# All attention values in one Strassen stage, through DRAM, in a hybrid decoder layer

## The chip, the cores and the metric

The kernel runs on one core of one Trainium2 chip. The metric is the time of one execution on the device in microseconds (us), lower is better. Beside plain timed runs there is one execution recorded by the hardware profiler, from which all rows below come. Its engines are PE (TensorE; PEld is its weight load), DVE (VectorE), ACT (ScalarE), POOL (GpSimd) and SP (SyncE, which issues most DMAs).

## The reference

One decoder layer on 1024 tokens of 1024 channels, float32. The part that matters here is the combined projection and the two attentions that read it:

```python
h = rms_norm(x, pre_mix_g[l])
proj = h @ w_in[l]
qa, ka, va, qb, kb, vb, gates = jnp.split(proj, split_at, axis=-1)
...
oa = diff_attention(qa, ka, va, lam)             # A: 4 heads, values 4 x 128 columns
oa = rms_norm(oa, diff_head_g[l]) * (1.0 - lam_init)
...
for g, (window, dil) in enumerate(B_PAIRS):      # B: 3 groups of 4 heads, values 3 x 512 columns
    o_g, lse_g = dilated_group(qb[:, :, g], kb[:, :, g], vb[:, :, g], window, dil)
...
mix = (g_a * ya + g_b * yb) @ w_mix_out[l]
x = x + rms_norm(mix, post_mix_g[l])
h = rms_norm(x, pre_ffn_g[l])                    # then a conv-gated MLP and a last residual
```

The values `va` and `vb` are 512 + 1536 = 2048 columns of `h @ w_in`: a product of 1024 x 1024 by 1024 x 2048.

## The kernel before, in words

Every float32 operand of a product is split into two fp32r parts, high and low: `split` writes the high part with a copy on ACT (whi, xh, t2h and so on) and the low part, source minus high, on DVE (wlo, xl, t2l). A product is then three matmuls, high by high, low by high and high by low (`mm3`), summed in PSUM. `xh` and `xl` hold the normalized input, transposed, as 8 blocks of 128 channels by 1024 tokens.

The stages, in order of time: three gate columns while x arrives (the "first" gates); the norm's factors `rstd`, their row form `rstd_row`, and the rotation tables; two more gate columns; the values of attention A's first head pair (`proj_v`, 65 to 87 us); query and key of head 0 (`proj_a`); attention A head by head (about 118 to 450 us); attention B in 12 steps of one (head pair, group, head) each (450 to 930); the output products; the mix; the MLP's up products, most by Strassen's scheme with seven products in place of eight; and the down products, likewise.

In the attentions a head is cut in blocks of 128 queries. A block makes scores (PE into PSUM `s`), takes the maximum with a mask (DVE), the exponential (ACT), combines (DVE), is transposed (PE into `pt`), split again (ACT, DVE) and multiplied with the values `vh`, `vl` (PE into `o`). Jobs that are due a block or two later are put off by `later`. Between these jobs, `interleave` spreads "fills", PE work that waits for nothing of the attention: the projections of the next head (`p`, in B `proj_b`), gate columns (`g`), and pieces of the value products (`v`, `w`, `V`, and in B the two halves of `values_of`). The strings in `A_FILLS` say which fills each of A's four heads gets. A head half of A closes with `head_norm`: PE sums squares into `o`, DVE computes a root and writes `spread`, PE transposes `spread` into `pt`, and DVE multiplies `osb` by that.

`proj_v` makes 256 columns at a time, token block by token block: 8 blocks of 8 x 3 matmuls of 256 columns. For A, and for B's group 0, the result goes straight from PSUM into `vh` and `vl`. For groups 1 and 2, whose keys are read with a stride, it goes through DRAM (`v_d`) and comes back permuted (`vperm`).

What sets the order: the code is written in the order of the stages, and a scheduler with a timeline of its own puts the instructions into each engine's queue, by priority and by when it takes operands to be there. Each engine then runs its queue strictly in order. PSUM has eight banks: `acc` has 3, `s` and `pt` 2 each, `o` 1. A gate column (`gate`, `put_gate`) is two half products of 24 matmuls into `acc`; DVE empties each with a multiply by `rstd_row`, and the result is stored to DRAM.

Of the kernel before, what the change touches and what calls it, by code (L numbers as in the profile page):

```python
# [24 lines left out]
P = 128  # L25
S = 1024
# [23 lines left out]
START_GATES, A_FILLS, B_GATES = 2, ("pggg", "pvgg", "wpgg", "PVg"), 3  # L50
# [8 lines left out]
def plan():  # L59

    order = [("t", GT + i * P) for i in FIRST_GATES]
    for pair in range(2):
        for h in (2 * pair, 2 * pair + 1):
            order += [("t", QA + h * P), ("t", KA + h * P)]
            if h % 2 == 0:
                order += [("v", VA + pair * 256, i) for i in range(2)]
    for pair in range(2):
        for g in range(BG):
            order += [("v", VB + g * 512 + pair * 256, i) for i in range(2)]
            for h in (2 * pair, 2 * pair + 1):  # L70
                order += [("t", QB + g * 512 + h * P), ("t", KB + g * 512 + h * P)]
    order += [("t", GT + i * P) for i in range(2 * KC) if i not in FIRST_GATES]
    return order
# [15 lines left out]
def trunk(ctx: ExitStack, tc: tile.TileContext, a, out):  # L89
# [28 lines left out]
    def load_raw(src):  # L118
        raw = raws_in[-1].tile([P, 512], F32, tag="raw", name="raw")
        dma(raw, src)  # L120
        return raw
# [71 lines left out]
    v_d = dram.tile([4, S, 256], F32, name="v_d")  # L193
# [15 lines left out]
    def proj_t(col, evacuate):  # L209

        wh, wl = load_unit(w_in[where[("t", col)]])
        for half, sl in enumerate(halves()):
            ps = psum()
            for k in range(KC):
                w = slice(k * P, (k + 1) * P)
                mm3(ps, wh[:, w], wl[:, w], xh[:, k, sl], xl[:, k, sl], k == 0, k == KC - 1)
                if k == KC - 1:
                    evacuate(half, sl, ps)
                if k % 2:
                    yield 0.5  # L220

    def put_gate(i, sl, ps):
        t = rt.tile([P, 512], F32, tag="t2", name="gate")
        nc.vector.tensor_tensor(t, ps, rstd_row[:, sl], op=ALU.mult)
        nc.scalar.dma_start(gt_d[i][:, sl], t)

# [46 lines left out]
    rt = open_pool(attn, "rt", side="right", bufs=2)  # L273
    raws_in.append(rt)
    ps_s = open_pool(attn, "ps_s", bufs=2, space=PSUM)
    ps_o = open_pool(attn, "ps_o", space=PSUM)
    tabs = open_pool(attn, "tabs", side="right")
    rstd_row = tabs.tile([P, S], F32, name="rstd_row")
    slots = open_pool(attn, "slots", side="right")
# [38 lines left out]
    with ExitStack() as st0:  # L318
# [6 lines left out]
        def load_first(c0, c1):  # L325
            for n, i in enumerate(FIRST_GATES):
                dma(raws[n][:, c0:c1], w_in[where[("t", GT + i * P)]][:, c0:c1])
# [73 lines left out]
        cos_a, sin_a = load_tabs(64, 32)  # L401
# [24 lines left out]
    def v_tiles(i):  # L426
        return [slot(t, (P, 4, 256)) for t in ("vh", "vl")]

    def proj_v(col, res, wk=None, via=None, dil=1, ms=range(8)):

        us = [load_unit(w_in[where[("v", col, i)]]) for i in range(2)]
        for m in ms:
            ps = psum()[:, :256]
            tk = slice(m * P, (m + 1) * P)
            for k in range(KC):
                wh, wl = us[k // 4]
                w = slice((k % 4) * 256, (k % 4 + 1) * 256)
                nc.tensor.matmul(ps, xh[:, k, tk], wh[:, w], start=k == 0, stop=False)  # L438
                nc.tensor.matmul(ps, xl[:, k, tk], wh[:, w], start=False, stop=False)  # L439
                nc.tensor.matmul(ps, xh[:, k, tk], wl[:, w], start=False, stop=k == KC - 1)  # L440
                if k == KC // 2 - 1:
                    yield 0.5
            r = rstd[:, m : m + 1]
            if via is None:
                if m % 4 == 0:
                    res.append(v_tiles(m // 4))
                h, l = (t[:, m % 4] for t in res[-1])
                nc.scalar.activation(h, ps, AF.Copy, scale=r)
                nc.vector.scalar_tensor_tensor(l, ps, r, h.bitcast(F32), op0=ALU.mult, op1=ALU.subtract)
            else:  # L450
                if m % 2 == 0:
                    vr = wk.tile([P, 2, 256], F32, tag="vraw", name="vraw", bufs=2)
                nc.scalar.activation(vr[:, m % 2], ps, AF.Copy, scale=r)
                if m % 2:
                    nc.scalar.dma_start(via.rearrange("(m p) c -> p m c", p=P)[:, m - 1 : m + 1], vr)
            yield 0.5
        if via is not None:
            n = S // dil // P
            src = via.rearrange("(ih p r) c -> p r ih c", r=dil, ih=n)
            for i in range(2):  # L460
                v = slot("vperm", (P, 4 // n, n, 256), F32)
                for ih in range(n):
                    dma(v[:, :, ih], src[:, i * 4 // n : (i + 1) * 4 // n, ih])
                h, l = v_tiles(i)
                split(h, l, v.rearrange("p r ih c -> p (r ih) c"))
                res.append((h, l))
# [160 lines left out]
    free_gates = [i for i in range(2 * KC) if i not in FIRST_GATES]  # L627

# [32 lines left out]
    def values_of(pair, g):  # L661
        col = VB + g * 512 + pair * 256
        if g == 0:
            return proj_v(col, vs_b[pair, g])
        return proj_v(col, vs_b[pair, g], wk_b[0], v_d[pair * 2 + g - 1], DIL[g])
# [5 lines left out]
    with st_a:  # L671
        ops = [[] for _ in range(AH)]
        vs = [[] for _ in range(AH // 2)]
        run(gates(START_GATES)[0])
        run(proj_v(VA, vs[0]))
        run(proj_a(0, ops[0]))
        for h in range(AH):
# [4 lines left out]
                "v": lambda: (proj_v(VA + 256, vs[1], ms=range(4)), 4),  # L682
                "w": lambda: (proj_v(VA + 256, vs[1], ms=range(4, 8)), 4),
                "g": lambda: gates(1),
                "P": lambda: (proj_b(0, 0, ops_b[steps[0]]), 8),
                "V": lambda: (values_of(0, 0), 8),
# [177 lines left out]
    for n, (pair, g, h) in enumerate(steps[:-1]):  # L864
# [3 lines left out]
        if h % 2 == 0 and n + 2 < len(steps):  # L868
            ahead = values_of(*steps[n + 2][:2])
            fills.append((itertools.islice(ahead, 8), 4))  # L870
        elif h % 2:
            fills.append((ahead, 4))
# [219 lines left out]
    tt = {}  # L1092

    def new_sum(name, x, ys, eng=None):

        t = tt[name] = sums.tile([P, 4, 512], F32, tag=name, name=name)
        f = lambda v: v.bitcast(F32)
# [9 lines left out]
    def split_sum(name, to=None):  # L1107

        to = to or [xw.tile([P, 4, 512], F32R, tag=name + p, name=name + p) for p in "hl"]
        pieces.extend(functools.partial(split, *(t[:, k] for t in to), tt[name][:, k]) for k in range(4))  # L1110
# [3 lines left out]
    with ExitStack() as st_s:  # L1114
# [5 lines left out]
        new_sum("t2", b22, tt["t1"])  # L1120
        new_sum("t4", b21, tt["t2"])
# [122 lines left out]

    def tt(o, x, y, op=ALU.subtract):
        nc.vector.tensor_tensor(o, x, y, op=op)
# [175 lines left out]
def layout(inp):  # L1422
# [10 lines left out]
    for u in plan():  # L1433
        if u[0] == "t":
            us.append(units(w[:, u[1] : u[1] + P], KC, P))
        else:
            us.append(units(w[u[2] * 512 : (u[2] + 1) * 512, u[1] : u[1] + 256], 4, 256))
    arr["w_in"] = np.stack(us)
    for n in ("w_a_out", "w_b_out"):
        arr[n] = np.stack([units(f[n][0][:, i * 256 : (i + 1) * 256], 4, 256) for i in range(4)])  # L1440
# [28 lines left out]
```

## Time and profile before

| | us |
|---|---|
| runs, median of 3 (lowest to highest) | 1772.2 (1769.66 to 1774.67) |
| profiled execution, its own time | 1767.12 |
| its span, first to last instruction | 1765.3 |
| PE busy in the span | 1721.8 |
| DVE busy | 1329.9 |
| ACT busy | 865.3 |

Busy time is the time in which at least one of the engine's instructions was running. A row of the timeline has the start of an instruction, how long it ran, engine, line, operation, and output and inputs by the program's names; a bracket at its end tells how long the engine stood before it and what released it. A row of groups has the count, the busy time, the mean of one in ns, and the idle time ahead of the group. Rows of stages have the busy time of each engine with its number of instructions, then the clock that PE was granted (1.00 is full), then DMA's share and GB/s.

### The profile page before, as it was taken

The page shows a single profiled execution, that of the slowest core. Times are in us where ns is not written, and L with a number is a line of the kernel's source. Part 1 is how long each engine was busy: PE and PEld are TensorE (multiplying, and loading weights), DVE is VectorE, ACT ScalarE, POOL GpSimd, SP SyncE. Part 2 cuts the span into 40 slices and gives each one's busy share as a digit, 9 for nine tenths or more (in the row PEclk, how much of TensorE's full clock was granted, in tenths as well). Part 3 has the DMA queues.
Part 4 walks back from the last instruction along what each step waited for, and adds up shares of the span by engine and source line. Part 5 has one row for each costly group of instructions (what it writes and reads, how often), then busy time and mean ns, then how long its engine had stood idle before and what let it go on. Part 6 is the DMA issues. An engine that isn't in the chain of part 4 may idle for free.

```text
span 1765.3 us, 24106 instructions
## 1 busy us (share of the span) xinstructions
PE 1721.8 (98%) x8754; PEld 1459.4 (83%) x8754; DVE 1329.9 (75%) x2612; ACT 865.3 (49%) x1585; POOL 51.6 (3%) x78
## 2 busy tenths in 40 slices
PE   9999999999999999999999999999999999999997
PEld 7987788789888888888877878878888888888886
DVE  4667786776556667565665867799999999789978
ACT  6375464644455645465652533364444444355452
POOL 0000000000000000000000410300000000000000
PEclk9999999999999999999999999999999999999999
DMA  8411112211121335221376533023222222196624
GB/s 271 162 60 42 54 55 72 78 55 59 56 86 60 102 97 156 75 88 55 126 254 222 166 131 108 37 72 107 90 78 95 78 78 96 60 342 216 206 77 155
DMA packets 100407, 197.61 MB, mean 112 GB/s; under 512 B 16368, under 2 KB 23216, under 8 KB 100288
## 3 DMA queue, kind: packets, MB, share of 16 engines
q1 hardware_dynamic: 92192, 185.06, 31.4%
q10 hardware_dynamic: 8096, 11.01, 1.7%
q8 instruction: 68, 1.11, 0.3%
q14 instruction: 51, 0.42, 0.1%
HBM read 152.37 MB, written 43.66 MB: 111 GB/s over the span
## 4 chain that ended last, share of the span: by engine, by line
PE 78%; DVE 9%; DMA 7%; issue 3%; ACT 3%; SPq 1%; POOL 0%; DVEq 0%; ACTq 0%
PE acc L148 15%; PE acc L147 15%; PE acc L149 15%; PE acc L438 3%; PE acc L440 3%; PE acc L439 3%; PE acc L1301 3%; PE acc L1300 3%; PE acc L1302 3%; PE acc L990 2%; PE acc L991 2%; PE acc L989 2%; PE o L484 2%; PE pt L472 1%; DMA og<-og_d 1%
## 5 line engine op out<-in xcount | busy, mean ns | idle before, releaser
L147 PE MATMUL acc<-xh,whi 128*128 128x512 f32 x744 | 296.3, 399 | 4.7 <-DVE t L421 2.6
L148 PE MATMUL acc<-xh,wlo 128*128 128x512 f32 x744 | 296.9, 399 | 1.4 <-DVE wlo L140 1.4
L149 PE MATMUL acc<-xl,whi 128*128 128x512 f32 x744 | 294.6, 398 | 0.0
L143 ACT ACTIVATE whi<-raw 128x512 fp32r<-128x512 f32 (+1 forms) x258 | 158.8, 624 | 208.5 <-PE acc L149 125.2
L140 DVE TENSOR_TENSOR wlo<-raw,whi 128x512 fp32r<-128x512 f32 (+1 forms) x255 | 185.0, 732 | 47.3 <-ACT whi L143 45.8
L147 PEld LDWEIGHTS acc<-xh,whi 128*128 128x128 f32 x744 | 140.6, 189 | 33.6 <-ACT xh L342 3.2
L148 PEld LDWEIGHTS acc<-xh,wlo 128*128 128x128 f32 x744 | 140.8, 189 | 29.2 <-DVE wlo L140 1.6
L149 PEld LDWEIGHTS acc<-xl,whi 128*128 128x128 f32 x744 | 141.2, 190 | 28.7
L147 PE MATMUL acc<-mh,whi 128*128 128x512 f32 x400 | 156.5, 391 | 1.9 <-ACT whi L143 1.7
L148 PE MATMUL acc<-mh,wlo 128*128 128x512 f32 x400 | 156.3, 391 | 0.2 <-DVE wlo L140 0.2
L149 PE MATMUL acc<-ml,whi 128*128 128x512 f32 x400 | 156.1, 391 | 0.0
L438 PE MATMUL acc<-whi,xh 128*128 128x256 f32 x512 | 147.4, 288 | 0.0
L440 PE MATMUL acc<-wlo,xh 128*128 128x256 f32 x512 | 146.8, 287 | 0.0
L439 PE MATMUL acc<-whi,xl 128*128 128x256 f32 x512 | 146.7, 287 | 0.0
L420 ACT ACTIVATE t<-acc 64x512 f32<-64x512 f32 (+1 forms) x160 | 94.6, 591 | 44.8 <-PE acc L149 42.4
L1175 DVE TENSOR_TENSOR u<-acc,u 128x512 f32<-128x512 f32 x133 | 90.6, 685 | 25.7 <-PE acc L149 25.6
L143 ACT ACTIVATE whi<-s 128x512 fp32r<-128x512 f32 x76 | 47.2, 628 | 105.2 <-PE acc L149 96.0
L439 PEld LDWEIGHTS acc<-whi,xl 128*128 128x128 f32 x512 | 97.7, 191 | 0.7
L438 PEld LDWEIGHTS acc<-whi,xh 128*128 128x128 f32 x512 | 97.8, 191 | 0.6
L440 PEld LDWEIGHTS acc<-wlo,xh 128*128 128x128 f32 x512 | 97.7, 191 | 0.5
L147 PEld LDWEIGHTS acc<-mh,whi 128*128 128x128 f32 x400 | 75.5, 189 | 18.2 <-ACT whi L143 2.1
L148 PEld LDWEIGHTS acc<-mh,wlo 128*128 128x128 f32 x400 | 75.5, 189 | 16.2 <-DVE wlo L140 0.5
(313 smaller groups left out, 3867.4 us busy)
## 6 DMA issues: line engine op xcount, KB each, us to landing
raw<-in_w_in SPq DMA_DIRECT2D x126, 256.0 KB, 2.7
raw<-in_w_up SPq DMA_DIRECT2D x88, 256.0 KB, 2.6
raw<-c_d SPq DMA_DIRECT2D x48, 256.0 KB, 3.5
c_d<-c SPq DMA_DIRECT2D x22, 512.0 KB, 2.7
raw<-in_w_down SPq DMA_DIRECT2D x37, 256.0 KB, 3.6
gl<-gt_d SPq DMA_DIRECT2D x16, 512.0 KB, 5.8
gt_d<-gate ACTq DMA_DIRECT2D x26, 256.0 KB, 2.0
og_d<-osb SPq DMA_DIRECT2D x12, 512.0 KB, 4.4
```

The lines of the kernel that those rows point to most:

```text
L140: eng.tensor_tensor(lo, src, hi.bitcast(F32), op=ALU.subtract)
L143: nc.scalar.activation(hi, src, AF.Copy)
L147: nc.tensor.matmul(o, sh, mh, start=first, stop=False)
L148: nc.tensor.matmul(o, sl, mh, start=False, stop=False)
L149: nc.tensor.matmul(o, sh, ml, start=False, stop=last)
L420: nc.scalar.activation(t1[dst], ps[src], AF.Copy)
L438: nc.tensor.matmul(ps, xh[:, k, tk], wh[:, w], start=k == 0, stop=False)
L439: nc.tensor.matmul(ps, xl[:, k, tk], wh[:, w], start=False, stop=False)
L440: nc.tensor.matmul(ps, xh[:, k, tk], wl[:, w], start=False, stop=k == KC - 1)
L1175: nc.vector.tensor_tensor(to, made(p), x, op=ALU.add)
L1300: nc.tensor.matmul(banks[m], gh[:, tk], wh, start=f == 0, stop=False)
L1301: nc.tensor.matmul(banks[m], gl[:, tk], wh, start=False, stop=False)
```

## The change

All 2048 value columns are made in one stage, after the first gates and four more gate columns (two before) and ahead of attention A. The stage is the product of 1024 tokens by 1024 channels by 1024 columns, twice (`cp` 0 and 1), each by Strassen's scheme: seven products of 512 x 512 x 512 in place of eight. Each is 4 x 4 x 3 matmuls of 512 columns, into four banks at once.

The x side of the seven products needs four combinations of x's quarters. `less` and `less_sum` compute T1 to T4 on DVE ahead of the four gates; T2 to T4 get places of their own, T1 is put into the quarter `b12` of `xh`, `xl` once the gates have read it, and that quarter is loaded again late in the stage. The weight side is combined on DVE as it arrives (`ready_v`) from a second layout of the weights, `w_v`. `take_v` adds the products up in SBUF (`yv`), `stored` scales by `rstd` and stores to `v_d`. Before each use, `values` loads four pieces of 128 x 2 x 256 from `v_d` and splits them. So a fill `v`, `w` or `V` now holds no PE work, and its weight is 0. The fills of A become pgg, pvg, wpg, PVgg in place of pggg, pvgg, wpgg, PVg. The load of A's rotation tables moves behind the stage, and `rt`, the pool of raw weights and rotation temporaries (2 buffers of each), is opened behind it.

```diff
-START_GATES, A_FILLS, B_GATES = 2, ("pggg", "pvgg", "wpgg", "PVg"), 3
+START_GATES, A_FILLS, B_GATES = 4, ("pgg", "pvg", "wpg", "PVgg"), 3
...
-    v_d = dram.tile([4, S, 256], F32, name="v_d")
+    v_d = dram.tile([S, 2048], F32, name="v_d")
...
-    def proj_v(col, res, wk=None, via=None, dil=1, ms=range(8)):
-
-        us = [load_unit(w_in[where[("v", col, i)]]) for i in range(2)]
-        for m in ms:
-            ps = psum()[:, :256]
...
+    def less(o, x, y, d):
+
+        tt(o, f32(x[0]), f32(y[0]))
+        tt(d, f32(x[1]), f32(y[1]))
+        tt(o, o, d, ALU.add)
+
+    def less_sum(o, x, y):
+
+        tt(o, f32(x[0]), y)
+        tt(o, o, f32(x[1]), ALU.add)
+
+    temps = open_pool(st_r, "temps", side="right")
+    t1_raw = [temps.tile([P, 512], F32, tag=f"t1{k}", name="t1") for k in range(4)]
+    for k in range(4):
+        x11, x12, x21, x22 = ([t[:, k] for t in b] for b in (b11, b12, b21, b22))
+        d, e, o = (temps.tile([P, 512], F32, tag=n, name=n) for n in "deo")
+        less(t1_raw[k], x12, x11, d)
+        less_sum(e, x22, t1_raw[k])
+        split(t2[0][:, k], t2[1][:, k], e)
+        less(o, x22, x12, d)
+        split(t3[0][:, k], t3[1][:, k], o)
+        less_sum(e, x21, e)
+        split(t4[0][:, k], t4[1][:, k], e)
+    todo = [free_gates.pop(0) for _ in range(START_GATES)]
+    for i in todo:
+        for _ in gate(i):
+            pass
+
+    for k in range(4):
+        split(*(t[:, k] for t in b12), t1_raw[k])
+    t1 = b12
...
+        order_v = (("p1", b11), ("p5", t1), ("p6", t2), ("p7", t3), ("p3", b22), ("p2", b21), ("p4", t4))
+        todo = [(cp, p, x, k) for cp in range(2) for p, x in order_v for k in range(4)]
...
+        def stored(y, cp, i, j, m):
+
+            tb = j * 4 + m
+            nc.scalar.activation(y, y, AF.Copy, scale=rstd[:, tb : tb + 1])
+            nc.scalar.dma_start(v_d[tb * P : (tb + 1) * P, cp * 1024 + i * 512 : cp * 1024 + (i + 1) * 512], y)
...
+        for n, (cp, p, x, k) in enumerate(todo):
+            while fetched < min(n + 8, len(todo)):
+                fetch_v(fetched)
+                fetched += 1
+            while made < min(n + 5, len(todo)):
+                ready_v(made)
+                made += 1
...
+            for m in range(4):
+                tk = slice(m * P, (m + 1) * P)
+                mm3(banks[m], x[0][:, k, tk], x[1][:, k, tk], wh, wl, k == 0, k == 3)
+            if k == 3:
+                for m in range(4):
+                    take_v(cp, p, m, banks[m])
...
+    def values(col, dil, res, pieces=range(4)):
+
+        n = S // dil // P
+        src = v_d[:, col : col + 256].rearrange("(ih p r) c -> p r ih c", r=dil, ih=n)
+        for i in pieces:
+            if i % 2 == 0:
+                res.append([slot(t, (P, 4, 256)) for t in ("vh", "vl")])
+            raw = load_raw(src[:, i * 2 // n : (i + 1) * 2 // n, 0] if n == 1 else src[:, i * 2 // n, 2 * i % n : 2 * i % n + 2])
+            split(*(t.rearrange("p b c -> p (b c)")[:, i % 2 * 512 : (i % 2 + 1) * 512] for t in res[-1]), raw)
+            yield 0
...
-        run(gates(START_GATES)[0])
-        run(proj_v(VA, vs[0]))
+        run(values(0, 1, vs[0]))
         run(proj_a(0, ops[0]))
...
-            fills.append((itertools.islice(ahead, 8), 4))
+            fills.insert(0, (itertools.islice(ahead, 2), 0))
```

What this does to the queues is seen at three places.

DVE near the start, up to the first multiply that frees a bank of the free gates. L385 and L387 (L384 and L386 after) write `rstd` and `rstd_row`, the other rows of L29x and L30x are the rotation tables. Before:

```order
L385 COPY edge<-rxy 128x8
L296 TENSOR_SCALAR ang<-ang,edge 128x1024
L387 COPY rstd_row<-edge 128x1024
L298 TENSOR_SCALAR kk<-ang 128x1024
L299 TENSOR_SCALAR kk<-kk 128x1024
L300 SCALAR_TENSOR_TENSOR sin<-kk,ang 128x1024
L140 TENSOR_TENSOR wlo<-raw,whi 128x512
L301 SCALAR_TENSOR_TENSOR sin<-kk,sin 128x1024
L302 SCALAR_TENSOR_TENSOR sin<-kk,sin 128x1024
L140 TENSOR_TENSOR wlo<-raw,whi 128x512
L224 TENSOR_TENSOR gate<-acc,rstd_row 128x512
```

After; L432 is `tt`, `e` and `t_484` are T sums, L136 splits them:

```order
L432 TENSOR_TENSOR e<-xh,t_484 128x512
L299 SCALAR_TENSOR_TENSOR cos<-kk,ang 128x1024
L384 COPY edge<-rxy 128x8
L432 TENSOR_TENSOR e<-e,xl 128x512
L300 SCALAR_TENSOR_TENSOR cos<-kk,cos 128x1024
L386 COPY rstd_row<-edge 128x1024
L136 TENSOR_TENSOR t2l<-e,t2h 128x512
L301 SCALAR_TENSOR_TENSOR cos<-kk,cos 128x1024
L432 TENSOR_TENSOR e<-xh,e 128x512
L303 TENSOR_SCALAR cos<-cos 128x1024
L395 SCALAR_TENSOR_TENSOR neg<-sin,pt 128x512
L220 TENSOR_TENSOR gate<-acc,rstd_row 128x512
```

`rstd_row` and the first multiply now come behind nearly all the T sums and behind the table of the cosine, which stood after the multiply.

DVE where the values end and the first query projection begins. L421 (L419) is the first operation on the finished query product; `wlo` ahead of it are that product's weights. Before:

```order
L449 SCALAR_TENSOR_TENSOR vl<-acc,edge,vh 128x256 x6
L140 TENSOR_TENSOR wlo<-raw,whi 128x512 x2
L449 SCALAR_TENSOR_TENSOR vl<-acc,edge,vh 128x256
L140 TENSOR_TENSOR wlo<-raw,whi 128x512 x2
L421 TENSOR_TENSOR t_914<-acc,cos 128x512
```

After; the `yv` rows are the additions of the stage's last two products:

```order
L432 TENSOR_TENSOR yv<-acc,yv 128x512 x3
L432 TENSOR_TENSOR yv<-o,yv 128x512
L432 TENSOR_TENSOR yv<-s,yv 128x512 x2
L432 TENSOR_TENSOR yv<-pt,yv 128x512 x2
L136 TENSOR_TENSOR vl<-raw,vh 128x512 x4
L136 TENSOR_TENSOR wlo<-raw,whi 128x512 x6
L419 TENSOR_TENSOR t_2227<-acc,cos 128x512
```

Two splits of the query's weights stood ahead of the last value evacuation; now all of them stand behind the last product's additions and behind four splits of values.

PE at the end of a head of A (head 1), up to the transposes of `spread` that close its first head half. Before:

```order
L484 MATMUL o<-pt,vh 128x2x128
L486 MATMUL o<-pt,vl 128x128
L486 MATMUL o<-pt,vl 128x256
L149 MATMUL acc<-xl,whi 128x512
L147 MATMUL acc<-xh,whi 128x512
L148 MATMUL acc<-xh,wlo 128x512
L149 MATMUL acc<-xl,whi 128x512
L147 MATMUL acc<-xh,whi 128x512
L148 MATMUL acc<-xh,wlo 128x512
L149 MATMUL acc<-xl,whi 128x512
L620 MATMUL pt<-ident,spread 128x128 x4
```

After:

```order
L593 MATMUL o<-pt,vh 128x512
L595 MATMUL o<-pt,vl 128x256
L593 MATMUL o<-pt,vh 128x512
L593 MATMUL o<-pt,vh 128x2x128
L595 MATMUL o<-pt,vl 128x128
L595 MATMUL o<-pt,vl 128x256
L647 MATMUL s<-k_3102,q_3100 128x512
L648 MATMUL s<-l_3104,q_3100 128x512
L729 MATMUL pt<-ident,spread 128x128 x4
```

The fills (`acc` rows) that stood between attention's products and these transposes are gone from this place; attention's own products follow one another.

180 lines of the change are left out of this document (105 added, 75 removed).

## The prediction

> **What bounds the kernel now.** I read the busy times first, then the chain of waits, then start-to-start times in the timeline, then stages. One caution: busy time counts a matmul from its start to its modelled end, and the next one starts long before that.
>
> ```profile
> PE 1721.8 (98%) x8754; PEld 1459.4 (83%) x8754; DVE 1329.9 (75%) x2612; ACT 865.3 (49%) x1585; POOL 51.6 (3%) x78
> PE 78%; DVE 9%; DMA 7%; issue 3%; ACT 3%; SPq 1%; POOL 0%; DVEq 0%; ACTq 0%
> ```
>
> TensorE (PE) is busy 98% of the span and carries 78% of the chain that ended last. So whatever PE no longer does is time won, as long as nothing else takes its place. The stages say how much room that leaves (columns: stretch, then the busy time of PE, PEld, DVE, ACT, POOL, and the granted clock):
>
> ```profile
> 118.00:190.50 72.50, 64.90 (x303) 53.05 (x302) 58.72 (x169) 44.58 (x88) 0.00 (x0) 0.93 0.11 37
> 190.50:449.90 259.40, 256.29 (x1466) 224.46 (x1465) 192.44 (x542) 131.81 (x267) 1.59 (x4) 0.99 0.19 63
> 450.00:930.00 480.00, 472.35 (x2814) 413.61 (x2813) 296.82 (x671) 270.22 (x561) 0.00 (x0) 1.00 0.33 108
> ```
>
> The first two are attention A, the third attention B. VectorE (DVE) stands at 81%, 74% and 62% while PE is nearly full. In A, DVE is the engine that is next, and PE's fill work is what hides it.
>
> **Part 1, the products.** Removed: 8 groups x 8 token blocks x 8 x 3 = 1536 products of 256 columns. Added: 2 column pairs x 7 products x 4 x 4 x 3 = 672 of 512 columns.
>
> ```profile
> L147 PE MATMUL acc<-xh,whi 128*128 128x512 f32 x744 | 296.3, 399 | 4.7 <-DVE t L421 2.6
> L438 PE MATMUL acc<-whi,xh 128*128 128x256 f32 x512 | 147.4, 288 | 0.0
> 14.01 0.39 PE L147 MATMUL acc<-xh,whi 128*128 128x512 f32 x1
> 14.69 0.39 PE L148 MATMUL acc<-xh,wlo 128*128 128x512 f32 x1
> 69.92 0.28 PE L438 MATMUL acc<-whi,xh 128*128 128x256 f32 x1
> 70.04 0.28 PE L439 MATMUL acc<-whi,xl 128*128 128x256 f32 x1
> ```
>
> By durations (288 and 399 ns) the change would save 1536 x 0.288 - 672 x 0.399 = 174 us. But those overlap: starts are 0.120 us apart at 256 columns and 0.2265 at 512 (the two rows shown are three starts, 0.68 us, apart). So PE gives up 1536 x 0.120 = 184.3 and takes on 672 x 0.2265 = 152.2: **-32.1 us**. The Trainium skill, TensorE: Matmul & The Clock Gate, section Back-to-back issue gap, gives N / 2.4 + 2.5 ns for a warm matmul by itself, 109 and 216 ns here; by it the saving would be 22.7 us. The rows lie 11 ns above it in both cases, and the sum goes by the rows.
>
> **Part 2, the start.** PE begins the gates of the first free group where it did, and now has four of them, 8 half products of 24 matmuls (5.44 us). They use 3 PSUM banks, and a bank is freed by a multiply with rstd_row. In front of rstd_row and that multiply DVE's queue now holds the sums and splits of the T matrices.
>
> ```profile
> 40.05 0.69 DVE L376 COPY gate<-acc 128x512 f32<-128x512 f32 x1 [7.82 <-PE acc L149]
> 46.18 0.17 DVE L167 TENSOR_TENSOR rxw<-rxy 128x8 f32<-128x8 f32 x1
> 46.38 0.17 DVE L168 TENSOR_TENSOR rxw<-rxw,rxv 128x8 f32<-128x8 f32 x1
> 51.52 0.69 DVE L387 COPY rstd_row<-edge 128x1024 f32<-128x1024 f32 x1
> 52.12 0.69 DVE L298 TENSOR_SCALAR kk<-ang 128x1024 f32<-128x1024 f32 x1
> 52.84 0.69 DVE L299 TENSOR_SCALAR kk<-kk 128x1024 f32<-128x1024 f32 x1
> 55.31 1.22 DVE L301 SCALAR_TENSOR_TENSOR sin<-kk,sin 128x1024 f32<-128x1024 f32 x1
> 56.56 1.23 DVE L302 SCALAR_TENSOR_TENSOR sin<-kk,sin 128x1024 f32<-128x1024 f32 x1
> 57.71 0.69 DVE L140 TENSOR_TENSOR wlo<-raw,whi 128x512 fp32r<-128x512 f32 x1
> 58.31 0.68 DVE L224 TENSOR_TENSOR gate<-acc,rstd_row 128x512 f32<-128x512 f32 x1
> 42.57 0.39 PE L147 MATMUL acc<-xh,whi 128*128 128x512 f32 x1
> 53.90 1.03 PE L394 MATMUL pt<-ident,rstd_row 128*128 128x128 f32 x8
> 54.69 0.47 PE L149 MATMUL acc<-xl,whi 128*128 128x512 f32 x1
> ```
>
> The first COPY waits for PE at 40.05 in either version. From it to the first gate multiply the changed order has 35 operations of 512 columns (0.60 start to start), 6 two-operand ones of 1024 (1.2), 9 one-operand ones of 1024 (0.70) and 13 small ones (0.20): 21.0 + 7.2 + 6.3 + 2.6 = 37.1 us, against 18.3 here. The first multiply thus runs near 40.05 + 0.6 + 37.1 + 0.6 = 78.4, plus a little for splits that wait for ScalarE (ACT). PE has filled its 3 banks at 42.57 + 3 x 5.44 = 58.9, does 0.8 us of transposes and stands until about 79: **+19 us**. Ends: 12 if ACT and DVE overlap better than I see, 25 if the splits wait.
>
> On SP's queue the first loads of w_v stand behind the stores of the rotation tables, which that order ends near 85 us. Ten loads of 256 KB at the 271 GB/s of the page's first slice take 10 us, so they land before the gates end, near 79 + 5 x 5.44 = 106; the gates are their cover.
>
> ```profile
> GB/s 271 162 60 42 54 55 72 78 55 59 56 86 60 102 97 156 75 88 55 126 254 222 166 131 108 37 72 107 90 78 95 78 78 96 60 342 216 206 77 155
> ```
>
> Passing from gates to the first product: its weights are split by ACT behind a DMA issue that waits for the last gate's multiply, so one multiply and one ACT split, **+1.5** (0 to 5).
>
> **Part 3, inside the values stage** I cost nothing more. Per 152 us DVE has 56 splits, 32 weight sums, 56 additions from PSUM and 4 restorations of xl, 148 x 0.60 = 89 us, and it works five weight tiles ahead of PE, 5 x 12 x 0.2265 = 13.6 us. The cover is PE's products; if DVE fell behind by those 13.6 us, the excess would show.
>
> **Part 4, from values to attention.** Four value pieces and then the first query weights are loaded through the 2 buffers of pool rt, and their splits stand on DVE and ACT behind the last product's additions and scalings. From PE's last product: last addition and scaling 1.5; two ACT splits with their DVE part 1.9; a load of the third and fourth piece 2.7; their splits 0.6 + 0.6; the weight load, which needs those buffers, 2.7; an ACT split 0.6.
>
> ```profile
> raw<-in_w_in SPq DMA_DIRECT2D x126, 256.0 KB, 2.7
> L143 ACT ACTIVATE whi<-raw 128x512 fp32r<-128x512 f32 (+1 forms) x258 | 158.8, 624 | 208.5 <-PE acc L149 125.2
> ```
>
> Overlap of pairs takes off a little: **+10 us** (7 to 14). After both long stops PE restarts at half rate, as at the beginning of this trace:
>
> ```profile
> 9.50 0.63 PE L148 MATMUL acc<-xh,wlo 128*128 128x512 f32 x1
> 12.06 0.63 PE L148 MATMUL o<-xh,wlo 128*128 128x512 f32 x1
> ```
>
> These are 6 starts apart, 0.43 us each; seven at 0.43 instead of 0.2265 cost 1.4 us: **+3** for two stops (0 to 5).
>
> **Part 5, attention A.** Its fill loses the value products and, net, two gates; DVE's attention work stays. Each head half ends in a closed pair, whose place is a head's end or the start of the next head: DVE writes spread, PE transposes it, DVE multiplies osb. Seven stretches lie between the eight pairs, from the first to the last of these rows:
>
> ```profile
> 190.45 0.68 DVE L621 TENSOR_TENSOR osb<-pt,osb 128x512 f32<-128x512 f32 x1
> 449.91 0.69 DVE L621 TENSOR_TENSOR osb<-pt,osb 128x512 f32<-128x512 f32 x1 [0.48 <-PE pt L620]
> ```
>
> I summed the rows of each stretch at their start-to-start times (for DVE before, that gives 194.9 us where the stage's row has 192.4). PE's work was 38.7, 36.6, 37.7, 33.8, 45.9, 31.6, 20.9 (245) and becomes 32.8, 11.8, 48.6, 14.3, 31.6, 10.4, 28.6 (178). DVE's work from one osb to the next spread was 14.4, 29.2, 16.3, 30.6, 15.4, 21.4, 6.5 and becomes 14.7, 22.3, 19.0, 21.7, 14.8, 24.7, 13.2. Before, PE had more to do in every stretch. Now DVE has more in the second, fourth and sixth: neither can pass the other there, so PE stands for 10.5 + 7.4 + 14.3 = 32 us at least. The upper end comes from the end of the first head, where the fills have run out in this trace too:
>
> ```profile
> 160.00:170.00 10.00, 6.66 (x38) 5.00 (x36) 6.95 (x24) 5.34 (x12) 0.00 (x0) 0.99 0.07 26
> 170.00:180.00 10.00, 7.63 (x34) 6.28 (x35) 7.45 (x25) 5.18 (x13) 0.00 (x0) 0.67 0.00 0
> 180.00:190.00 10.00, 8.10 (x41) 6.38 (x40) 8.66 (x43) 5.27 (x15) 0.00 (x0) 0.84 0.02 7
> 240.00:250.00 10.00, 10.00 (x78) 9.60 (x76) 9.84 (x25) 7.47 (x17) 0.00 (x0) 1.00 0.10 29
> ```
>
> There DVE did 23.1 us of work in 30, because the softmax passes back and forth between engines. At that rate the three stretches take 68.7 / 0.77 = 89 us, 53 over PE's 36. I take **+45**, nearer the like stretch than the floor; ends 25 and 55. For the first head, which loses 5 us of fill ahead of the first pair, **+2** (0 to 5).
>
> **Part 6, attention B.** It loses five value groups, 115 us of PE work. Twelve steps keep some 27 us of PE work against 21 of DVE, so PE still leads; value loads now wait on SP for rt's buffers with weight loads behind them, and at the change of head pair one step has 14.5 against 21.9. **+5** (0 to 15; the upper end is A's idle share before, 11 of 332 us, on 370 us, and a little).
>
> **Sum.** -32.1 + 19 + 1.5 + 10 + 3 + 45 + 2 + 5 = +53. The profiled execution took 1767.1 us (span 1765.3), so 1820; the median shown is 1772.2, 0.3% above it, so 1825 on that footing. I predict 1822.
>
> **Rivals.**
> - *DVE's idle quarter absorbs it* (faster). DVE is idle for 435 us and gets about 100 us more work; at 240 to 250 it ran at 98% with PE full. If the start's sums and the head ends cost PE nothing, the sum is -32.1 + 1.5 + 10 + 1.5 = -19, some 1753. It decides in A's three stretches and at the start: together they must cost under 20 us. Against it: the order fixes who stands ahead of whom.
> - *Attention stays bound by PE, only the start stops* (same): -32.1 + 19 + 1.5 + 10 + 3 = +1, some 1774. Against it: the three stretches.
> - *The clock falls in the emptied head ends* (slower still). At 170 to 190 the clock averaged 0.67 and 0.84, which lost 5 us of PE rate in one head end; four such ends, with PE slow also into the next head's projections, add 20 to the sum: 1842. The Trainium skill, same page, section The HAM clock gate, says that idle stretches of about 3.4 us drop PE to half its clock, and that it takes about as long a busy stretch to bring it back. By that rule the emptied ends run at half clock throughout; the rows above agree in direction.
>
> **Chances.** The sum as it stands 0.68, clock 0.17, same 0.08, faster 0.07. The first two bring slower to 0.85, and half of the same case ends a little above 0.3% (about what a measurement here can tell from no change): faster 0.07, same 0.05, slower 0.88. The range 1788 to 1852 runs from A at its lower end with small stops (-32 + 12 + 7 + 25 + 4 = +16, on the median) to the clock's case with B at its end; under 2 in 10 lie outside.
>
> **What would show it.** Right: PE idle for 15 to 25 us before 80 us, released by DVE's gate multiply; a gap of about 10 us between the last value product and the first query product, released by ACT's split; PE idle ended by spread or by attention's DVE and ACT work at head ends, the granted clock under 0.9 there; 672 value products spaced 0.2265. Wrong: gates without a gap, or under 205 us from the first osb multiply to the last (259.4 before; 192 if only PE counted). Then I have mispriced DVE's queue, or PE passes what I take for closed.

## The result, and the profile after

The changed kernel takes **1873.6 us** (median of 4 runs, 1869.7 to 1875.0) against 1771.9 for the kernel before in the same session: a ratio of **1.057, 95% interval 1.0547 to 1.0593**. It is slower by about 102 us. I had predicted slower, but 1822 and at most 1852: the direction was right, the size half of what came.

The profiled execution's span is 1873.1 us, 107.8 more than before. First the page's busy times and its shares of the chain of waits:

```profile
PE 1734.1 (93%) x7890; PEld 1431.1 (76%) x7890; DVE 1427.8 (76%) x2772; ACT 903.6 (48%) x1633; POOL 51.3 (3%) x78
PE 67%; DVE 14%; DMA 8%; ACT 6%; issue 4%; SPq 1%; POOL 0%; DVEq 0%; ACTq 0%
```

PE was at 98% and is at 93%; its share of the chain fell from 78 to 67%, and what came in is DVE, ACT and DMA. PE's idle time grew by 96 us ((1873.1 - 1734.1) - (1765.3 - 1721.8)). Where it lies, by stages (stretch, then busy time of PE, PEld, DVE, ACT, POOL; granted clock; DMA share; GB/s):

```profile
0.00:57.90 57.90, 54.66 (x223) 44.33 (x224) 47.44 (x79) 32.99 (x54) 4.14 (x9) 0.97 0.73 248
57.90:79.50 21.60, 4.85 (x18) 3.57 (x17) 21.60 (x40) 7.84 (x10) 0.00 (x0) 0.63 0.03 12
79.50:106.40 26.90, 26.90 (x117) 21.92 (x115) 8.87 (x14) 2.54 (x4) 0.00 (x0) 0.98 0.43 140
106.40:114.70 8.30, 0.07 (x1) 0.00 (x0) 2.68 (x5) 0.63 (x1) 0.00 (x0) 0.80 0.95 276
114.70:269.00 154.30, 154.25 (x672) 127.32 (x672) 91.76 (x144) 64.84 (x105) 0.82 (x2) 0.99 0.41 134
269.00:287.10 18.10, 0.01 (x1) 0.01 (x1) 3.48 (x7) 4.64 (x8) 0.00 (x0) 0.58 0.58 196
287.10:388.20 101.10, 92.42 (x410) 74.88 (x411) 76.70 (x193) 63.69 (x118) 0.00 (x0) 0.92 0.13 42
388.20:624.70 236.50, 207.29 (x992) 170.64 (x991) 174.78 (x514) 122.42 (x247) 0.00 (x0) 0.91 0.18 60
624.70:1041.90 417.20, 380.62 (x1872) 317.79 (x1871) 284.47 (x657) 244.90 (x515) 1.60 (x4) 0.94 0.32 104
1041.90:1873.10 831.20, 813.06 (x3595) 670.62 (x3593) 715.99 (x1128) 359.08 (x574) 44.71 (x63) 0.99 0.37 127
```

The fifth row is the new stage: 672 matmuls in 154.3 us with PE full, as priced. The second, fourth and sixth are three stops around it, the third the rest of the four gates, the seventh head 0's projections and its first half. The last three are attention A from its first `osb` multiply to the start of B, attention B, and the rest. In A and B PE is no longer full, and the granted clock is 0.91 and 0.94, where it was 0.99 and 1.00.

The three stops (the first in two rows) and one of B's, in the timeline (the bracket: how long PE stood, and what released it):

```profile
73.39 1.97 PE L393 MATMUL pt<-ident,rstd_row 128*128 128x128 f32 x8 [14.58 <-DVE rstd_row L386]
77.53 0.80 PE L143 MATMUL acc<-xh,whi 128*128 128x512 f32 x1 [2.17 <-DVE gate L220]
114.72 0.80 PE L143 MATMUL acc<-whi,xh 128*128 128x512 f32 x1 [8.24 <-ACT whi L139]
287.09 1.22 PE L143 MATMUL acc<-xh,whi 128*128 128x512 f32 x2 [18.12 <-ACT whi L139]
787.05 1.22 PE L143 MATMUL acc<-xh,whi 128*128 128x512 f32 x2 [5.28 <-ACT whi L139]
```

B's stop at 787 is one of a kind: in B's 12 steps PE stood six times for over 3 us, four times for `whi` and twice for `osb`. What leads to this one, on SP, ACT, SP and ACT:

```profile
755.94 1.01 SPq L116 DMA_DIRECT2D raw<-v_d  x2
781.37 1.15 ACT L139 ACTIVATE vh<-raw 128x512 fp32r<-128x512 f32 x2
783.44 4.64 SPq L116 DMA_DIRECT2D raw<-in_w_in  x3
786.37 1.27 ACT L139 ACTIVATE whi<-raw 128x512 fp32r<-128x512 f32 x2 [1.87 <-DMA raw<-in_w_in]
```

Two value pieces are loaded early in the step, at 755.94, into the two raw buffers of `rt`. ACT splits them only at 781.37, at the step's end. Till then they hold both buffers, so the first weights of the next projection can be loaded only at 783.44; they are split at 786.37, and PE begins at 787.05.

### The profile page after: what moved, and what is told of

Read it like the earlier page. It is cut to its first block, busy times and chain, and to the rows that moved or that the text cites. A ratio compares the mean times of both kernels' runs of the same rounds, so it can differ in the third digit from the quotient of the medians.

```text
span 1873.1 us, 22818 instructions
## 1 busy us (share of the span) xinstructions
PE 1734.1 (93%) x7890; PEld 1431.1 (76%) x7890; DVE 1427.8 (76%) x2772; ACT 903.6 (48%) x1633; POOL 51.3 (3%) x78
## 4 chain that ended last, share of the span: by engine, by line
PE 67%; DVE 14%; DMA 8%; ACT 6%; issue 4%; SPq 1%; POOL 0%; DVEq 0%; ACTq 0%
PE acc L143 14%; PE acc L144 14%; PE acc L145 14%; PE acc L1401 2%; PE acc L1400 2%; PE acc L1402 2%; PE acc L1093 2%; PE acc L1094 2%; PE acc L1092 1%; DMA gl<-gt_d 1%; DMA raw<-in_w_in 1%; ACT t L418 1%; DMA og<-og_d 1%; PE s L143 1%; PE s L144 1%
## 5 line engine op out<-in xcount | busy, mean ns | idle before, releaser
L143 PE MATMUL acc<-xh,whi 128*128 128x512 f32 x744 | 302.9, 410 | 47.1 <-ACT whi L139 40.9
L144 PE MATMUL acc<-xh,wlo 128*128 128x512 f32 x744 | 301.2, 405 | 0.6 <-DVE wlo L136 0.6
L139 ACT ACTIVATE whi<-raw 128x512 fp32r<-128x512 f32 (+1 forms) x238 | 146.4, 623 | 215.8 <-PE acc L145 88.3
L136 DVE TENSOR_TENSOR wlo<-raw,whi 128x512 fp32r<-128x512 f32 (+1 forms) x235 | 172.6, 743 | 80.1 <-ACT whi L139 70.8
L143 PEld LDWEIGHTS acc<-mh,whi 128*128 128x128 f32 x400 | 75.5, 189 | 18.1 <-ACT whi L139 1.9
L145 PEld LDWEIGHTS acc<-ml,whi 128*128 128x128 f32 x400 | 75.4, 189 | 15.5
L419 DVE TENSOR_TENSOR t<-acc,cos 128x512 f32<-128x512 f32 x64 | 44.1, 690 | 43.8 <-ACT t L418 42.8
L1401 PE MATMUL acc<-whi,wlo 128*128 128x512 f32 x220 | 77.3, 389 | 0.0
L593 PE MATMUL o<-pt,vh 128*128 128x512 f32 (+1 forms) x188 | 63.2, 402 | 15.1 <-DVE osb L875 9.5
L1400 PE MATMUL acc<-whi 128*128 128x512 f32 x220 | 75.8, 389 | 0.0
L1402 PE MATMUL acc<-wlo,whi 128*128 128x512 f32 x220 | 72.9, 389 | 0.0
```

Of the source, the lines that this page charges most:

```text
L136: eng.tensor_tensor(lo, src, hi.bitcast(F32), op=ALU.subtract)
L139: nc.scalar.activation(hi, src, AF.Copy)
L143: nc.tensor.matmul(o, sh, mh, start=first, stop=False)
L144: nc.tensor.matmul(o, sl, mh, start=False, stop=False)
L145: nc.tensor.matmul(o, sh, ml, start=False, stop=last)
L419: nc.vector.tensor_tensor(t2, ps, cos[:, sl], op=ALU.mult)
```

## The experiments

Each kernel below is the changed one with the edit shown. Ratios are to the kernel before, timed on the same chip; its median was 1769 to 1773 us in these sessions, so a difference between two of the kernels is known to some 3 us at best.

### Buffers of their own for the value pieces

```diff
-            raw = load_raw(src[...])
+            raw = rt.tile([P, 512], F32, tag="vraw", name="vraw", bufs=2)
+            dma(raw.rearrange("p (b c) -> p b c", c=256), src[...])
-SLOTS = 18
+SLOTS = 17
```

> The value pieces of both attentions get two raw buffers of their own in pool rt, in place of the two that the weights use; to make room the operand ring has 17 slots, not 18. Theory A (the value pieces hold the weights' two buffers until the end of a step, so each step of attention B begins with a late weight): PE's waits for whi in attention B, 22.3 us in 8 waits, fall under 6 us, the granted clock of B rises from 0.94 to 0.97 or more, B shrinks from 417 us to 380-392, and the kernel to 1835-1850 us. Theory B (attention's own chain has lost its cover, and the late weight is only where it shows): other waits take their place, B stays above 405 us and the kernel above 1860.

Measured: 1809.6 us, ratio 1.021 (1.0186 to 1.0234): 64 us less, more than theory A asked for. A and B, by stages:

```profile
379.00:611.90 232.90, 209.57 (x1015) 172.77 (x1014) 178.45 (x524) 123.76 (x250) 0.00 (x0) 0.94 0.19 62
611.90:973.30 361.40, 356.16 (x1853) 300.63 (x1853) 277.58 (x652) 240.00 (x509) 1.69 (x4) 1.00 0.36 115
```

The end of the stop ahead of A, in its timeline:

```profile
279.66 1.22 PE L143 MATMUL acc<-xh,whi 128*128 128x512 f32 x2 [10.29 <-ACT whi L139]
```

B went from 417 to 361 us with the clock at 1.00, and the stop ahead of A from 18.1 to 10.3. B's loss was thus not in its chain of scores, softmax and values: that chain is unchanged here. My 380 to 392 was too cautious since it counted only the waits named for `whi`, not the slow clock behind them and other waits that became shorter with them (`o` for `osb`: 9.5 us in the changed kernel's B, 3.9 here).

The ring of 17 slots alone (the second part of that diff) as a control:

> Control for the run with the value pieces' own buffers: only the operand ring is cut from 18 to 17 slots, the value pieces still share the weights' two buffers. Theory A (the buffers made the 64 us, not the ring): 1870 to 1882 us, attention B within 8 us of 417. Rival (the ring's other turn let the pieces be split earlier): under 1850 us.

Measured: 1877.9 us, ratio 1.0612 (1.0593 to 1.0632). The ring gave nothing; the buffers did.

### The value pieces in another place, without more buffers

```diff
-        fills = [(proj_b(nxt[1], nxt[2], ops_b[nxt]), 8)]
+        proj = proj_b(nxt[1], nxt[2], ops_b[nxt])
+        fills = [(itertools.islice(proj, 4), 4), (proj, 4)]
...
-            fills.insert(0, (itertools.islice(ahead, 2), 0))
+            fills.insert(1, (itertools.islice(ahead, 2), 0))
...
-            fills.insert(0, (ahead, 0))
+            fills.insert(1, (ahead, 0))
```

> No buffer is added: in attention B the two value pieces of a step are written between the query's and the key's projection of the next step, not ahead of both. Theory A (the shared buffers stand full of value pieces over the step's end): the query's weights are then split ahead of the value pieces and PE is not kept from them; the key's weights wait instead, but with 10.9 us of query products as cover. PE's waits for whi in B fall from 22.3 us under 12, B from 417 to 385-402, the kernel to 1840-1860 us. Theory B (two buffers are too few wherever the pieces stand): the waits move to the key's weights, B within 8 us of 417, the kernel within 8 us of 1873.

Measured: 1877.6 us, ratio 1.0602 (1.0583 to 1.0620). Theory B holds. PE's waits in B, of the changed kernel and then of this one (us, times, longest), and this one's B as a stage:

```profile
PE acc L143 <- ACT whi L139: 22.3, 8, 5.3
PE o L593 <- DVE osb L875: 9.5, 4, 4.3
```

```profile
PE acc L143 <- ACT whi L139: 10.7, 5, 4.0
PE o L593 <- DVE pt L136: 7.7, 3, 2.6
PE pt L581 <- ACT bs L846: 4.2, 6, 1.7
```

```profile
626.60:1047.90 421.30, 386.53 (x1875) 320.22 (x1874) 286.52 (x662) 244.24 (x520) 1.48 (x4) 0.94 0.33 106
```

The wait named `whi` halved and others took its place; B stayed at 421 us. So it is the number of buffers for two streams that helps, and not this other order in which the streams use them. And a wait that halves under its name is no time won.

### Gates as fill in attention A

```diff
-START_GATES, A_FILLS, B_GATES = 4, ("pgg", "pvg", "wpg", "PVgg"), 3
+START_GATES, A_FILLS, B_GATES = 2, ("pggg", "pvgg", "wpgg", "PVg"), 3
```

> Two gates stay at the start instead of four, and attention A gets back the gates that it had in the kernel before (8 in place of 6). Theory A (PE stands idle in A's head ends because its fill is gone): the 2 x 10.9 us of products leave the start and fall into A's idle time, A stays at 236 us within 6, kernel 1851-1860 us. Theory B (DVE's attention work sets A's pace and gates add DVE and PSUM work to it, or the fills sit where PE is full anyway): A grows by 12 to 22 us and the kernel stays within 8 us of 1873.

Measured: 1850.7 us, ratio 1.0448 (1.0426 to 1.0469), 23 us less, the whole 21.8 of the two gates. First and last `osb` multiply of A, in the changed kernel and here:

```profile
L730 DVE TENSOR_TENSOR osb<-pt,osb x8: 681/684/692, 388.2 to 624.0; 128x512 f32<-128x512 f32 x8
```

```profile
L730 DVE TENSOR_TENSOR osb<-pt,osb x8: 679/681/692, 369.0 to 605.1; 128x512 f32<-128x512 f32 x8
```

A takes 235.8 us with six gates and 236.1 with eight. In A PE really stood idle, and two gates of fill were worth their full time there.

### The T sums behind `rstd_row`

```diff
+        for t in (t1_raw[k], o):
+            nc.vector.tensor_copy(t[:, :1], rstd_row[:, :1])
         less(t1_raw[k], x12, x11, d)
```

> The T sums are made to wait for rstd_row by eight one-column copies, so they stand behind the chain that makes rstd_row. Theory A (the stall at the start is DVE's queue in front of rstd_row): rstd_row is written near 53 us instead of 72.7, PE's stop of 14.6 us before 73 us is gone, the gates end near 88 instead of 106. Since the stage's weight loads wait for the memory of the sums, the first value product comes 8 to 16 us earlier, not the full 17, and the kernel at 1857-1866 us. Theory B (the sums are needed before the first products in any order, so the stall only moves): first value product as before at 115 us or later, kernel within 4 us of 1873.

Measured: 1879.1 us, ratio 1.0604 (1.0585 to 1.0623).

```profile
48.99 0.69 DVE L386 COPY rstd_row<-edge 128x1024 f32<-128x1024 f32 x1
113.79 0.79 PE L143 MATMUL acc<-whi,xh 128*128 128x512 f32 x1 [27.38 <-ACT whi L139]
```

`rstd_row` comes 24 us earlier and the gates do not stop. But the first value product comes at 113.79 instead of 114.72, after one stop of 27.4 us in place of 16.8 and 8.2. DVE now makes the T sums beside the gates and behind them. Its last split of a sum, then the stage's first weight loads on SP:

```profile
109.30 0.69 DVE L136 TENSOR_TENSOR t4l<-e,t4h 128x512 fp32r<-128x512 f32 x1 [0.69 <-ACT t4h L139]
110.02 1.76 SPq L485 DMA_DIRECT2D wa<-in_w_v  x4
```

In the changed kernel these loads are issued at 106.75, behind the last gate's multiply. They go to memory that the sums and the gates give back (a run below moves them). So DVE's queue made the stop where I had put it, but the sums must end before the stage in either order, and the stop only moved. That is theory B, with a first product 1.2 us earlier and a time 2 us longer than it allowed. The longer time is not the sums': the first `osb` multiply comes 2.2 us earlier than in the changed kernel (386.0 against 388.2), and A takes 242.2 us instead of 235.8.

A takes 6 to 8 us longer in three runs whose edits do not touch it, this one and the next two. In each of the three the scheduler wrote A in another order: up to the second `osb` multiply the trace has 116 to 118 fill products on PE, against 105 in the changed kernel and, in the same order, in the control with 17 slots. That this order costs the 6 to 8 us was not tried alone.

### The first query weights ahead of the first value pieces

```diff
-        run(values(0, 1, vs[0]))
         run(proj_a(0, ops[0]))
+        run(values(0, 1, vs[0]))
```

> The first query and key projections are written ahead of the first four value pieces. Theory A (the 18.1 us between the last value product and the first query product are the way of the value pieces through the two buffers, v_d's stores included): PE restarts after the rotation tables' loads, one weight load (2.9 us) and one split, 6 to 9 us after the last value product; kernel 1861-1866 us, the values' way being covered by 21.7 us of projection products. Theory B (the wait returns at attention's first product with values): gap short, but the first osb multiply comes at the same distance, kernel within 4 us of 1873.

Measured: 1882.2 us, ratio 1.0621 (1.0593 to 1.0648): slower than either theory said. The stop ahead of A fell from 18.1 to 10.0 us, but new waits came:

```profile
PE s L647 <- ACT k L621: 11.5, 3, 6.3
```

Scores now wait for the key operand `k`, and the first `osb` multiply comes at 392.2 instead of 388.2. A itself takes 243.3 instead of 235.8 us, in another order, as just said.

### Plain products in place of Strassen's

```diff
-        order_v = (("p1", b11), ("p5", t1), ("p6", t2), ("p7", t3), ("p3", b22), ("p2", b21), ("p4", t4))
-        todo = [(cp, p, x, k) for cp in range(2) for p, x in order_v for k in range(4)]
+        todo = [(cp, i, j, k) for cp in range(2) for i in range(2) for j in range(2) for k in range(KC)]
...
-                mm3(banks[m], x[0][:, k, tk], x[1][:, k, tk], wh, wl, k == 0, k == 3)
+                mm3(banks[m], xh[:, k, tk], xl[:, k, tk], wh, wl, k == 0, k == KC - 1)
```

> The stage makes the same values by plain products of 512 columns, 768 instead of 672, with no T sums, no weight sums, no additions from PSUM and no second making of xl; all else is as in the changed kernel. This parts Strassen's scheme from the moving. By my prices: 96 x 0.2265 = +21.7 us of products; the stop of 14.6 + 2.2 us before the gates goes, -17; so +5, the kernel at 1872-1884 us. Rival: the stop at the start is only moved (as in the run with the sums later), so the saving is under 8 us and the kernel is at 1885-1895. Other rival: with the sums' memory gone, the first product's weights are there when the gates end and 8 us more go: 1866-1872.

Measured: 1856.0 us, ratio 1.0479 (1.0460 to 1.0498): 17.5 us faster than with Strassen's scheme, below all three expectations. The places of the first and the third stop as stages, then what is left of the second in the timeline:

```profile
57.90:79.50 21.60, 21.60 (x97) 17.86 (x96) 15.36 (x21) 3.50 (x3) 0.00 (x0) 1.00 0.53 192
265.00:270.00 5.00, 5.00 (x24) 4.14 (x23) 1.39 (x2) 3.89 (x7) 0.00 (x0) 1.00 0.47 141
```

```profile
89.01 0.50 PE L143 MATMUL acc<-whi,xh 128*128 128x512 f32 x1 [1.87 <-ACT whi L139]
94.43 0.79 PE L143 MATMUL acc<-whi,xh 128*128 128x512 f32 x1 [2.38 <-ACT whi L139]
```

Of the three stops 16.8, 6.4 and 18.1 us are gone and one of 2.4 is new: 39 us less, for the 21.7 us of products that Strassen's scheme saves. The first `osb` multiply comes 20.9 us earlier (367.3); A, in its other order, takes 241.5 us and gives 5.7 of that back. I had not seen the third stop as Strassen's. T2 to T4 lie in SBUF to the last product, and A's pools (`rt`, the tables, the slots) are opened behind them; without them the loads for A run during the stage. That it is this memory, and not the additions behind the last product, is read from the trace and was not tried alone.

### The gains together

The diff of the buffers with that of the gates:

> The value pieces' own buffers and the two gates in attention A together. If the two times lost are of different places, the gains add up: 1809.6 - 22.9 = 1787, 1782 to 1792 us. If both fill the same idle time of PE, under half of the second is left: over 1797 us.

Measured: 1793.1 us, ratio 1.0125 (1.0097 to 1.0152): 80 us under the changed kernel, where the two alone give 64 and 23. That is more than the 75 us at most if both filled the same idle time, but 1 us outside the range I gave for adding up; the spread of its runs is 1787.1 to 1798.8.

And on top of these, another place for the first product's weights:

```diff
+    wv = open_pool(st_w, "wv")
     temps = open_pool(st_r, "temps", side="right")
...
-        wv = open_pool(st_w, "wv", side="right")
```

> As the run with buffers and gates, and the tiles for the first product's weights lie in other memory, so that their loads wait for the first stage's tiles and not for the T sums and the gate tiles. Theory: the 11 us between gates and first product are the wait for that memory and a load; the first product comes 6 to 10 us earlier, kernel 1777-1781 us. Rival: SyncE's queue or DVE's splits behind the sums set it: within 3 us of the run with buffers and gates.

Measured: 1787.2 us, ratio 1.0102 (1.0080 to 1.0124). In the trace the stop ahead of the first product is 4.0 instead of 10.3 us; the two ratios' intervals overlap, so of the time nothing is shown, and neither forecast is met. The stop was partly the wait for that memory.

Next the diffs of plain products, buffers and gates in one kernel:

> Plain products in the stage, the value pieces' own buffers (17 slots) and two gates moved from the start to attention A. If the three gains are of separate places they add up: 1856 - 64 - 23 = 1769, 1763 to 1777 us, which is the kernel before within its spread. Rival (two of them fill the same idle time): over 1780 us.

Measured: 1783.4 us, ratio 1.0075 (1.0062 to 1.0087): the rival, 14 us over the sum. Part of the buffers' gain was counted twice: they had shortened the stop ahead of A by 7.8 us, and by plain products that stop is gone anyway. And with two gates at the start there is a new stop ahead of the first product, since the loads of `w_v` stand on SP behind the rotation tables' stores. SP, then PE:

```profile
68.74 0.36 SPq L399 DMA_DIRECT2D tab_d<-cos  x1
69.16 3.28 SPq L116 DMA_DIRECT2D raw<-in_w_v  x6
```

```profile
75.84 0.80 PE L143 MATMUL acc<-whi,xh 128*128 128x512 f32 x1 [11.24 <-ACT whi L139]
```

The same with none and with one gate at the start:

```diff
-START_GATES, A_FILLS, B_GATES = 2, ("pggg", "pvgg", "wpgg", "PVg"), 3
+START_GATES, A_FILLS, B_GATES = 0, ("pggg", "pvggg", "wpggg", "PVg"), 3
```

```diff
+START_GATES, A_FILLS, B_GATES = 1, ("pggg", "pvgg", "wpggg", "PVg"), 3
```

> As the run before in this list, with no gate at the start and ten in attention A. Attention A had 9 us of PE idle and a granted clock of 0.94 with eight gates, so it can take perhaps 15 of the 21.8 us of two more: theory A, 1750 to 1762 us, faster than the kernel before. Rival (without gates at the start PE waits for the first value weights from 43 us on, and A is full): 1766 us or more.

> As the run with no gate at the start, with one there and nine in attention A. Theory A (idle time in A is the limit): between the two runs above, 1757 to 1768 us. Rival (the first value weights are late and one gate covers them): below the run with none, 1750 to 1756 us.

Measured: with one gate 1776.6 us, ratio 1.0038 (1.0026 to 1.0051), over its expectation. With none **1763.5 us, ratio 0.9971 (0.9960 to 0.9982)**: a little over theory A's range, and faster than the kernel before by 0.3%, about the least that can be told. Why one gate is worse than none was not followed up. The first load of `w_v` in the run with none, and its A and B by stages:

```profile
44.15 0.33 SPq L116 DMA_DIRECT2D raw<-in_w_v  x1
```

```profile
321.20:571.20 250.00, 241.28 (x1194) 201.92 (x1193) 187.76 (x535) 127.82 (x256) 0.00 (x0) 0.97 0.23 73
571.20:927.80 356.60, 351.92 (x1839) 296.01 (x1838) 274.87 (x650) 236.61 (x506) 1.15 (x4) 1.00 0.36 117
```

The first `w_v` load is issued 25 us earlier than with two gates, and A takes ten gates in 250.0 us, against eight in 236.5 in the run with two gates at the start: 13.5 of the 21.8 us of the two more are paid now, so A is nearly full. One stage of 512-column products can thus hold its own, but by plain products, with buffers of its own and ten gates as A's fill. The kernel before was not tried with its gates in other places, so this does not compare the two ways at their best.

## Why the prediction was wrong

The terms, against the trace (us):

| step | predicted | measured | how |
|---|---|---|---|
| products | -32.1 | -32.1 | 672 matmuls in 154.3, nearly all at 0.2265, the first eight slower |
| stop before and in the gates | +19 | +16.8 | 14.58 + 2.17 |
| gates to first product | +1.5 (0 to 5) | +8.2 | bracket at 114.72 |
| values to attention | +10 (7 to 14) | +18.1 | bracket at 287.09 |
| first head | +2 | +2.8 | 101.1, less 103.3 - 5 |
| attention A | +45 | +43.4 | 235.8, less 259.4 - 67 |
| attention B | +5 (0 to 15) | +53.8 | 417.9, less 479.3 - 115.2 |
| after B | 0 | -4.9 | 831.2, less 836.1 |

These sum to +106.1 of 107.8. The slow restarts, +3 for two in the forecast, have no row of their own: by the starts after each stop they cost 1.6 us in the gates, 1.7 in the values stage and 2.5 in the first head, whose row holds the last. Why the part after B is 4.9 us shorter stays open.

**Attention B is the step that failed.** "Value loads now wait on SP for rt's buffers with weight loads behind them" named the mechanism, and the run with buffers of their own shows that it is nearly all of the term: B at 361.4 us has lost 118, hardly more than the 115 of its products. The price was wrong: +5, at most +15, for what measured +53.8. I had taken its upper end from the idle share of A before, a stage in which no value piece goes through these buffers. Rows that stood in the prediction give an estimate per change of step: a load (2.7), an ACT split (0.6) and seven restarts at half rate (1.4) are 4.7, and eleven changes make 52. That it comes so near is in part luck: by steps PE's idle time in B is 0 to 5.9 us, not 3.3 each. I had counted "PE still leads" over the whole step, though PE can lead only with work whose weights are there. Before, the code put the value products just there, at a step's end.

**The two hand-overs** were too small by 6.7 and 8.1. For both I followed the queues of ACT, DVE and SP, and left out memory: these loads wait for tiles that others give back. The first product's weights go where sums and gate tiles lay, and other memory for them made that stop 6.3 us shorter. A's tables are issued from 269.0 us on, when the last product has read T4, and the value pieces follow at 275.2 and the weights at 283.4. In the plain run, where that memory is free, the whole third stop and 6.4 of the 8.2 are gone.

**What held.** The start was put right in place and size, though the run with the sums later shows that undoing it alone wins nothing. A was right in size and in kind. The second, fourth and sixth of its seven stretches, from one `osb` multiply to the next, are these:

```profile
422.66:451.29 28.63, 18.10 (x86) 14.35 (x85) 23.24 (x76) 18.69 (x42) 0.00 (x0) 0.73 0.09 30
500.99:528.20 27.21, 21.60 (x105) 17.24 (x104) 22.73 (x76) 18.35 (x42) 0.00 (x0) 0.87 0.12 32
561.25:592.05 30.80, 18.74 (x87) 14.78 (x86) 23.99 (x81) 16.01 (x38) 0.00 (x0) 0.73 0.12 38
```

PE stands 10.5, 5.6 and 12.1 us in them (the floor was 10.5, 7.4 and 14.3), nearly always for DVE, and at most 0.6 in each of the other four. Together they take 86.6 us, near the upper end of 89. The clock fell in them, to 0.73 and 0.87, but within the +45. The value buffers hardly touch A: with buffers of its own it still takes 232.9 us.

The signs that the prediction named came in kind, the second gap at 18.1 us in place of 10. None had been named for B.

**The rivals.** "DVE's idle quarter absorbs it" and "only the start stops" fell with A and B. "The clock falls" had the right sign, at 1842 still 32 us short, and it looked at A's head ends alone: the slow clock that cost most, some 25 us, was B's. Each term that had a range came out within it, except B's, 39 us over its upper end, and the two hand-overs', 7 over theirs together. With B at its upper end the time would have been inside 1788 to 1852.

## What to carry to other kernels

Products that fill an attention do two things: they use PE, and they give the next weights time to arrive. Whoever moves them out must price each place where the next work now has to be there at once, as load + split + slow restart, times the number of such places, or give the next weights room to come early: with the value pieces out of their buffers B lost nothing here. A second stream through a pair of staging buffers needs buffers of its own; the one other order that was tried helped nothing. And a scheme that saves PE work by sums is also to be charged for making and holding them: here the stops that went with it were 39 us, for 21.7 us of products.

## What the runs showed of the hardware

A stop of 5.28 us in B had a slow restart behind it. Windows of 4 us around it, and the rows after it:

```profile
780.00:784.00 4.00, 1.51 (x8) 0.88 (x6) 3.67 (x11) 3.94 (x8) 0.00 (x0) 0.98 0.00 0
784.00:788.00 4.00, 0.95 (x2) 0.83 (x3) 3.80 (x14) 2.12 (x4) 0.00 (x0) 0.50 0.42 131
788.00:792.00 4.00, 4.00 (x15) 3.31 (x14) 2.89 (x4) 2.33 (x4) 0.00 (x0) 0.67 0.66 212
792.00:796.00 4.00, 4.00 (x25) 3.50 (x24) 1.83 (x11) 0.53 (x2) 0.00 (x0) 1.00 0.98 206
```

```profile
789.35 0.63 PE L145 MATMUL acc<-xl,whi 128*128 128x512 f32 x1
789.78 0.63 PE L143 MATMUL acc<-xh,whi 128*128 128x512 f32 x1
790.21 0.59 PE L144 MATMUL acc<-xh,wlo 128*128 128x512 f32 x1
790.63 0.40 PE L145 MATMUL acc<-xl,whi 128*128 128x512 f32 x1
790.87 0.39 PE L143 MATMUL acc<-xh,whi 128*128 128x512 f32 x1
```

The clock was 0.98 while PE began to stand, 0.50 in the next 4 us, and the matmuls after the stop start 0.43 us apart until 790.63, 3.6 us after the restart; then 0.23. The Trainium skill, TensorE: Matmul & The Clock Gate, section HAM oscillation, describes this as a loop that pays a cold start after every wait for data of over some 3.4 us; the trace agrees. Of the 54 us that B lost, PE's added idle time is only 29 (36.6 against 7.6 before). The other 25, by subtraction, are the slow clock: PE is busy for 380.6 us in B, against 356.2 in the run with buffers of their own, which makes the same products. There B has one stop of over 3 us, of 3.41, and its clock is 1.00.
